# A prologue with fixed instruction queues on three engines, without GpSimd, and with the scale columns as single-column products on TensorE

## The chip, the cores and the metric

The kernel runs on one core of a Trainium2 chip. The metric is the device time of one execution in microseconds (us); the median of three executions is given. Engines are named as in the profile: PE (TensorE), PEld (its weight loads), DVE (VectorE), ACT (ScalarE), POOL (GpSimd) and SP (SyncE, which issues most of the DMAs).

## The reference

One decoder block on a sequence of 1024 tokens with 1024 channels, one sequence, in float32. Two token mixers, a Conformer convolution and an mLSTM, run side by side on one input projection and are merged by gates; a SwiGLU feed-forward block and a final RMS norm follow. What matters here is the start:

```python
mod = silu(c) @ w_ada + b_ada              # (1, 6*1024), six rows of 1024
sh1, sc1, g1, sh2, sc2, g2 = split(mod, 6)
h = rms_norm(x, norm_mix_g) * (1 + sc1) + sh1
proj = h @ w_in + b_in                     # (1024, 10248)
a = proj[:, :1024] * sigmoid(proj[:, 1024:2048])   # then a 31-tap causal convolution
```

Before the first product of `h` with `w_in` can run, the kernel needs the mean square of each token, `x` transposed, and the two conditioning rows `sh1` and `sc1`, each a product of the vector `silu(c)` with a 1024 x 1024 part of `w_ada`.

## The kernel before

The kernel keeps `h` transposed: 8 tiles of 128 channels by 1024 tokens. To keep float32 accuracy at the speed of the faster product format, every operand is split into a high part in that format (`hh`, `whi`) and a low remainder (`hl`, `wlo`), and a product of two matrices becomes three: high by high, high by low, low by high. A block of 128 output channels (`wblock`, line 371) is 8 k-tiles x 3 products x 2 halves of 512 tokens, 48 products, into a two-bank accumulator `mm` of which there are two.

The order of instructions on each engine is chosen by the tile scheduler, which simulates the program with the place in the program as the priority. Code can fix an order with `queue_behind` (line 174), which makes one instruction follow another in its engine's queue without a semaphore wait. The prologue before uses none of that.

The prologue (lines 179 to 320) goes like this.

- Loads: `c`, the four `xt` tiles of `x` (1 MB each), `b_ada`, then the conditioning weights `wad` in four groups of 2 MB (`load_ada`, line 197, four DMAs each: halves of k by shift and scale), with the raw weights of the first two blocks between group 0 and group 1, and the raw weights of the next two blocks (`w_next`, line 217) after group 3. All are issued by SP.
- Mean squares on ACT (line 234), the power for the inverse root on POOL (line 105), the scaling of `xt` on DVE and ACT (line 243, 241), transposes on PE (line 247) and their evacuation to `xT` by ACT or DVE (lines 250 and 252, chosen by `EVAC`).
- The first weights `wf` are split by ACT (high) and POOL (low), lines 149 and 150.
- For each group g of two k-tiles: `mod_cols` (line 263) sums `wad` times `silu(c)` over the 8 k-tiles on DVE, shift and scale together, in eight steps over 128 x 512 (lines 271 and 273), folds the 128 partitions with four single-column products on PE (line 275), and ACT makes the columns `sh1` and `G1` (lines 278 and 279). Then ACT writes `hh` (line 309) and the full value over `xT` (line 313), and the remainder `hl` is subtracted on POOL for k-tiles 0 and 1 and on DVE for the others (line 314).
- `first_products` (line 281) adds the two k-tiles of a group into the accumulators of the first two blocks: 24 products of 128 x 512 a group. In the program those of group g-1 stand behind group g's columns.
- The parameter rows for later (`later`, line 296) share a buffer tag with the sums (`macc`).

After it `glu(1, w_next)` runs the next two blocks, whose weights had been loaded in the prologue and whose low parts POOL subtracts (`WN`). From then on the blocks follow each other, with the convolution taps on DVE put in between by `pump`.

Of the kernel before, what the change touches and what calls it, by code (L numbers as in the profile page):

```python
# [23 lines left out]
PUMP = 5500  # L24
# [25 lines left out]
def hybrid_block(ctx: ExitStack, tc: tile.TileContext, x, c, w_ada, b_ada, norm_mix_g, w_in, b_in,  # L50
                 conv_dw_w, conv_dw_b, conv_ln_g, conv_ln_b, w_conv_pw, b_conv_pw, qk_conv_w,
                 qk_conv_b, mlstm_norm_g, w_out, norm_ffn_g, w_ffn_up, w_ffn_down, final_norm_g, out):
    nc = tc.nc
    PSUM = bass.MemoryType.PSUM
    x2, out2 = x[0], out[0]
    wada, win, wpw, wo = w_ada[0], w_in[0], w_conv_pw[0], w_out[0]
# [81 lines left out]
    def load_raw(src, row0, kt, col0):  # L138
        raw = wp.tile([128, kt, 128], F32, name="wraw", tag="wraw")
        nc.sync.dma_start(raw, src[row0:row0 + kt * 128, col0:col0 + 128].rearrange("(k p) e -> p k e", p=128))  # L140
        return raw

    def load_split(src, row0, kt, col0, hi=None, lo=None, raw=None, eng=None):
        if raw is None:
            raw = load_raw(src, row0, kt, col0)
        if hi is None:
            hi = wp.tile([128, kt, 128], F32R, name="whi", tag="whi")
            lo = wp.tile([128, kt, 128], F32R, name="wlo", tag="wlo")
        nc.scalar.activation(hi, raw, AF.Copy)  # L149
        (eng or nc.vector).tensor_sub(lo, raw, hi.bitcast(F32))  # L150
        return hi, lo
# [43 lines left out]
    wad = []  # L195
# [29 lines left out]
    def dw_col(j, ct):  # L225
        r = j * 8 + ct
        return cols["dw0"][:, r:r + 1] if r < 128 else cols["dw1"][:, r - 128:r - 127]

    rstd = pro.tile([128, 3, 8], F32, name="rstd")
    xT = [big.tile([128, S], F32, name=f"xT{k}", tag="xb") if k < XB else pro.tile([128, S], F32, name=f"xT{k}") for k in range(KT)]  # L230
    for q in range(2):
        for t in range(4 * q, 4 * q + 4):
            junk = ps_mm()
            nc.scalar.activation(flat(junk), xt[t], AF.Square, accum_out=rstd[:, 0, t:t + 1])
        ms, rs, sc = (rstd[:, i, 4 * q:4 * q + 4] for i in range(3))
        nc.vector.tensor_scalar(ms, ms, 1.0 / D, EPS, op0=OP.mult, op1=OP.add)
        rsqrt(rs, ms)
        for t in range(4 * q, 4 * q + 4):
            r = rstd[:, 1, t:t + 1]
            if SCALE[t] == "a":  # L240
                nc.scalar.activation(xt[t], xt[t], AF.Copy, scale=r)
            else:
                (nc.gpsimd if SCALE[t] == "p" else nc.vector).tensor_scalar(xt[t], xt[t], r, None, op0=OP.mult)
        for k in range(KT):
            p = ps_n() if k % 3 == 0 else ps_c()
            for t in range(4):
                nc.tensor.transpose(p[:, t * 128:(t + 1) * 128], xt[q * 4 + t][:, k * 128:(k + 1) * 128], ident)
            h = xT[k][:, q * 512:(q + 1) * 512]
            if EVAC[q][k] == "a":
                nc.scalar.activation(h, p, AF.Copy)  # L250
            else:
                nc.vector.tensor_copy(h, p)

    first = [ps_mm(), ps_mm()]

# [7 lines left out]
    def mod_cols(g):  # L263
        p = ps_a()
        part = lambda t, i: t[:, i // 2, (i % 2) * 128:(i % 2) * 128 + 128]
        b = mod_b[:, g]
        acc = pro.tile([128, 2, 2, 256], F32, name="macc", tag="macc", bufs=MACC)
        for k in range(KT):
            a = acc[:, 0]
            if k < 1:  # L270
                nc.vector.tensor_scalar(a, wad[g][:, k], sc_c[:, k:k + 1], None, op0=OP.mult)
            else:
                nc.vector.scalar_tensor_tensor(a, wad[g][:, k], sc_c[:, k:k + 1], a, op0=OP.mult, op1=OP.add)
        for i in range(4):
            nc.tensor.matmul(p[:, i:i + 1], part(acc[:, 0], i), ones_col, start=True, stop=True)
        for i in range(2):
            k = 2 * g + i
            nc.scalar.activation(sh1[:, k:k + 1], p[:, i:i + 1], AF.Identity, bias=b[:, 0, i:i + 1])
            nc.scalar.activation(G1[:, k:k + 1], p[:, 2 + i:3 + i], AF.Identity, scale=mix_g[:, g, i:i + 1], bias=b[:, 1, i:i + 1])

    def first_products(g):
        ks = (2 * g, 2 * g + 1)
        steps = [(i, k, n, x) for n, x in ((0, hh), (1, hh), (0, hl)) for k in ks for i in range(2)]
        if g == 3:
            steps.sort(key=lambda step: step[0])
        for i, k, n, x in steps:
            for a, b in HALVES:
                nc.tensor.matmul(flat(first[i])[:, a:b], w_first[i][n][:, k, :], x[k][:, a:b], start=(g == 0 and k == 0 and n == 0 and x is hh),
                                 stop=(g == 3 and k == KT - 1 and x is hl))

    hl = []
    for g in range(4):
        mod_cols(g)
        if g == 2:
            rows = pro.tile([128, 8, 128], F32, name="rows", tag="macc", bufs=MACC)
# [11 lines left out]
        ks = (2 * g, 2 * g + 1)  # L307
        for k in ks:
            nc.scalar.activation(hh[k], xT[k], AF.Identity, bias=sh1[:, k:k + 1], scale=G1[:, k:k + 1])
        for k in ks:  # L310
            h = xT[k]
            hl.append(big.tile([128, S], F32R, name=f"hl{k}", tag="xb"))
            nc.scalar.activation(h, h, AF.Identity, bias=sh1[:, k:k + 1], scale=G1[:, k:k + 1])
            (nc.gpsimd if k in ON_POOL else nc.vector).tensor_sub(hl[k], h, hh[k].bitcast(F32))
        if g > 0:
            first_products(g - 1)
    first_products(3)
    for rows in later:
        param_columns(rows)
    prologue.close()  # L320
# [47 lines left out]
    cv = {}  # L368
    done = set()

    def wblock(col0, busy=PUMP, raw=None):
        w = load_split(win, 0, KT, col0, raw=raw, eng=WN if raw is not None else None)
        acc = ps_mm()
        for k in range(KT):
            mm_k(acc, k, KT, w, hh, hl)
            pump(busy / KT)
            yield
        return acc

    def run(steps):  # L380
        for _ in steps:
            pass
# [9 lines left out]
                next(filler, None)  # L392
                credit -= 1

    def glu(ct, raws=(None, None)):
        pb = yield from wblock(GLU_B + ct * 128, raw=raws[0])
        sg = glu_gate(ct, pb)
        pa = yield from wblock(ct * 128, raw=raws[1])
# [890 lines left out]
```

## Time and profile before

| what | value |
|---|---|
| median of three executions | 1737.80 us (1737.73 to 1738.36) |
| the profiled execution's own time | 1740.02 us |
| its span | 1738.3 us, 20880 instructions |
| PE busy, whole span | 1694.6 us (97%) |
| DVE, ACT, POOL busy, whole span | 1253.1, 612.6, 67.6 us |
| first hh product on PE (line 288) | 33.42 us |
| first product of the block after the prologue (line 159) | 67.98 us |
| DMA in the first 44 us | mostly 290 to 420 GB/s |

Times in the profile count from the start of the span. A line such as L273 is a line of the kernel, a group is all instructions of one line, engine and shape, and a pair `out<-in` names the tiles. `x8` is the number of instructions in a row or group. The granted clock is the share of PE's full clock that the throttle let through.

### The profile page before, as it was taken

The page shows a single profiled execution, that of the slowest core. Times are in us where ns is not written, and L with a number is a line of the kernel's source. Part 1 is how long each engine was busy: PE and PEld are TensorE (multiplying, and loading weights), DVE is VectorE, ACT ScalarE, POOL GpSimd, SP SyncE. Part 2 cuts the span into 40 slices and gives each one's busy share as a digit, 9 for nine tenths or more (in the row PEclk, how much of TensorE's full clock was granted, in tenths as well). Part 3 has the DMA queues.
Part 4 walks back from the last instruction along what each step waited for, and adds up shares of the span by engine and source line. Part 5 has one row for each costly group of instructions (what it writes and reads, how often), then busy time and mean ns, then how long its engine had stood idle before and what let it go on. Part 6 is the DMA issues. An engine that isn't in the chain of part 4 may idle for free. (4 is left out here: it accounts for less than half of the span.)

```text
span 1738.3 us, 20880 instructions
## 1 busy us (share of the span) xinstructions
PE 1694.6 (97%) x8360; PEld 1420.8 (82%) x8360; DVE 1253.1 (72%) x1673; ACT 612.6 (35%) x811; POOL 67.6 (4%) x119
## 2 busy tenths in 40 slices
PE   5999999999999999999999998999999999999998
PEld 4798888888888888888888788888888888878887
DVE  7888998997799669537798668766666665685243
ACT  6525335322522253223522376322223221332122
POOL 3100001000001000000000000000000000000000
PEclk8999999999999999999999999999999999999999
DMA  9111111121111111243595642322222222553121
GB/s 334 48 52 46 49 61 38 49 73 61 37 49 61 61 49 48 85 138 91 202 376 188 219 158 98 110 73 85 85 85 73 83 81 97 212 170 112 58 92 53
DMA packets 194711, 179.91 MB, mean 104 GB/s; under 512 B 7463, under 2 KB 166711, under 8 KB 194615
## 3 DMA queue, kind: packets, MB, share of 16 engines
q1 hardware_dynamic: 177367, 146.61, 27.3%
q10 hardware_dynamic: 17248, 31.99, 5.1%
q8 instruction: 65, 1.06, 0.2%
q14 instruction: 31, 0.25, 0.0%
HBM read 146.06 MB, written 32.51 MB: 103 GB/s over the span
## 5 line engine op out<-in xcount | busy, mean ns | idle before, releaser
L341 DVE SCALAR_TENSOR_TENSOR cacc<-a,col,cacc 128x1024 f32<-128x1024 f32 x240 | 305.6, 1280 | 4.7 <-ACT cacc L339 2.3
L159 PE MATMUL mm<-hh,wlo 128*128 128x512 f32 x864 | 271.5, 392 | 1.2 <-DVE wlo L150 1.2
L159 PE MATMUL mm<-hl,whi 128*128 128x512 f32 x864 | 271.9, 392 | 0.0
L159 PE MATMUL mm<-hh,whi 128*128 128x512 f32 x864 | 270.8, 392 | 0.8 <-ACT t L365 0.8
L159 PEld LDWEIGHTS mm<-hh,wlo 128*128 128x128 f32 x864 | 160.5, 188 | 33.5 <-DVE wlo L150 2.3
L159 PEld LDWEIGHTS mm<-hh,whi 128*128 128x128 f32 x864 | 160.4, 188 | 32.6 <-ACT t L365 1.2
L159 PEld LDWEIGHTS mm<-hl,whi 128*128 128x128 f32 x864 | 160.7, 188 | 32.1 <-issue 0.5
L149 ACT ACTIVATE whi<-wraw 128x1024 fp32r<-128x1024 f32 x62 | 65.7, 1060 | 225.0 <-PE mm L159 182.2
L150 DVE TENSOR_TENSOR wlo<-wraw,whi 128x1024 fp32r<-128x1024 f32 x60 | 73.1, 1218 | 22.2 <-ACT whi L149 18.8
L1066 PE MATMUL mm<-Bh,gh 128*128 128x512 f32 (+1 forms) x192 | 71.5, 374 | 3.6 <-ACT gh L1003 3.5
L1067 PE MATMUL mm<-Bl,gh 128*128 128x512 f32 (+1 forms) x192 | 71.5, 373 | 0.6 <-DVE Bl L985 0.6
L556 PE MATMUL mm<-wlo,hh 128*128 128x256 f32 x256 | 72.0, 282 | 0.0
L1068 PE MATMUL mm<-Bh,gl 128*128 128x512 f32 (+1 forms) x192 | 71.2, 371 | 0.0
L487 DVE SCALAR_TENSOR_TENSOR cacc<-qkraw,col,cacc 128x1024 f32<-128x1024 f32 x48 | 61.5, 1281 | 5.3 <-ACT cacc L485 4.6
L1255 DVE TENSOR_TENSOR x<-x,mm 128x1024 f32<-128x1024 f32 x24 | 29.2, 1217 | 50.0 <-PE mm L1253 48.0
L1131 ACT ACTIVATE whi<-wraw 128x512 fp32r<-128x512 f32 (+2 forms) x32 | 25.3, 790 | 111.8 <-PE mm L1253 69.9
L555 PE MATMUL mm<-whi,hh 128*128 128x256 f32 x192 | 54.4, 284 | 0.0
L557 PE MATMUL mm<-whi,hl 128*128 128x256 f32 x192 | 54.2, 283 | 0.0
L1252 PE MATMUL mm<-fa,wlo 128*128 128x512 f32 x128 | 50.1, 391 | 1.0 <-DVE wlo L1132 1.0
L1251 PE MATMUL mm<-fa,whi 128*128 128x512 f32 x128 | 49.9, 390 | 0.9 <-DVE cu L1094 0.9
L1004 DVE TENSOR_TENSOR ul<-uraw,uh 128x1024 fp32r<-128x1024 f32 x20 | 24.5, 1225 | 35.2 <-ACT uh L1003 35.2
L1253 PE MATMUL mm<-fa,whi 128*128 128x512 f32 x128 | 49.8, 389 | 0.0
(442 smaller groups left out, 3917.9 us busy)
## 6 DMA issues: line engine op xcount, KB each, us to landing
wraw<-in_w_in_dram SPq DMA_DIRECT2D x64, 512.0 KB, 4.2
awt<-in_w_ada_dram SPq DMA_DIRECT2D x32, 512.0 KB, 10.1
graw<-in_w_ffn_up_dram SPq DMA_DIRECT2D x24, 512.0 KB, 4.6
uraw<-in_w_ffn_up_dram SPq DMA_DIRECT2D x22, 512.0 KB, 14.5
draw<-in_w_ffn_down_dram SPq DMA_DIRECT2D x22, 512.0 KB, 4.4
act_d<-cg ACTq DMA_DIRECT2D x38, 256.0 KB, 2.2
wad<-in_w_ada_dram SPq DMA_DIRECT2D x16, 512.0 KB, 10.3
wraw<-in_w_out_dram SPq DMA_DIRECT2D x16, 512.0 KB, 3.9
```

Of the source, the lines that this page charges most:

```text
L149: nc.scalar.activation(hi, raw, AF.Copy)
L150: (eng or nc.vector).tensor_sub(lo, raw, hi.bitcast(F32))
L159: nc.tensor.matmul(flat(acc)[:, a:b], lhs[:, k, :], rhs[k][:, a:b], start=(first and k == 0), stop=(last and k == kt - 1))
L341: nc.vector.scalar_tensor_tensor(acc, a[:, j:j + S], dw_col(j, ct), acc, op0=OP.mult, op1=OP.add)
L487: nc.vector.scalar_tensor_tensor(cv, raw[:, j:j + S], wcol(j), cv, op0=OP.mult, op1=OP.add)
L555: nc.tensor.matmul(o, hh[k][:, ts_], his[k], start=False, stop=False)
L556: nc.tensor.matmul(o[:, 0:256], hh[k][:, ts_], los[k], start=False, stop=False)
L557: nc.tensor.matmul(o, hl[k][:, ts_], his[k], start=False, stop=(k == KT - 1))
L1066: nc.tensor.matmul(o, a, rh, start=(k == 0), stop=False)
L1067: nc.tensor.matmul(o, a, rl, start=False, stop=False)
L1068: nc.tensor.matmul(o, b, rh, start=False, stop=(k == 3))
L1252: nc.tensor.matmul(o, lo[:, i, :], his[i][:, a:b], start=False, stop=False)
```

## The change

- `ON_POOL`, `WF` and `WN` go: GpSimd does no subtraction in the prologue any more. The low parts of the first weights and all `hl` are subtracted on DVE.
- The conditioning sums are cut in two. The shift half stays as a sum on DVE (`shift_sums`, over 128 x 256), folded by two single-column products. The scale half is computed on PE directly: for each of the two columns of a group, eight products over k with the `wad` block as the stationary operand and one column of `silu(c)` as the moving one (`mod_products`).
- The full value of the even k-tiles goes to DVE, that of the odd ones stays on ACT.
- `first_products` is cut into the products with `hh` (kind 0, eight pairs) and those with `hl` (kind 1, four pairs).
- `in_turn` fixes the order of the listed groups on DVE (`on_v`), ACT (`on_s`) and PE (`on_t`).
- Only one raw tile of the next pair is loaded in the prologue, in the last group; its split comes last on ACT and DVE, and the pair's second block is loaded and split like any other.
- The parameter rows get their own tag of two buffers.

```diff
-ON_POOL = (0, 1)
-    rows = pro.tile([128, 8, 128], F32, name="rows", tag="macc", bufs=MACC)
+    rows = pro.tile([128, 8, 128], F32, name="rows", tag="rows", bufs=2)
...
-    WF = nc.gpsimd
-    WN = nc.gpsimd
-    w_first = []
+    w_first, raws = [], []
     for i in range(2):
-        w_hi, w_lo = (pro.tile([128, KT, 128], F32R, name=f"wf{i}{j}") for j in range(2))
-        w_first.append(load_split(win, 0, KT, GLU_B if i == 0 else 0, w_hi, w_lo, eng=WF))
+        w_first.append([pro.tile([128, KT, 128], F32R, name=f"wf{i}{j}") for j in range(2)])
+        raws.append(load_raw(win, 0, KT, GLU_B if i == 0 else 0))
...
-    w_next = [load_raw(win, 0, KT, GLU_B + 128), load_raw(win, 0, KT, 128)]
+
+    def split_rest():
+        for i in range(2):
+            load_split(None, 0, KT, 0, *w_first[i], raw=raws[i])
...
+            if q and k > 1:
+                late_evac[e].append(ins)
...
+    def in_turn(groups):
+        for a, b in zip(groups, groups[1:]):
+            for ins in b:
+                for earlier in a:
+                    queue_behind(ins, earlier)
+
+    def shift_sums(g):
+        acc = pro.tile([128, 256], F32, name="macc", tag="macc", bufs=MACC)
+        parts = [[], []]
+        for k in range(KT):
+            if k < 1:
+                ins = nc.vector.tensor_scalar(acc, wad[g][:, k, 0], sc_c[:, k:k + 1], None, op0=OP.mult)
+            else:
+                ins = nc.vector.scalar_tensor_tensor(acc, wad[g][:, k, 0], sc_c[:, k:k + 1], acc, op0=OP.mult, op1=OP.add)
+            parts[k // 4].append(ins)
+        return acc, parts
+
+    def mod_products(g, acc):
+        p = ps_a()
+        out = []
+        for i in range(2):
+            for k in range(KT):
+                out.append(nc.tensor.matmul(p[:, 2 + i:3 + i], wad[g][:, k, 1, i * 128:(i + 1) * 128], sc_c[:, k:k + 1],
+                                            start=(k == 0), stop=(k == KT - 1)))
+        for i in range(2):
+            out.append(nc.tensor.matmul(p[:, i:i + 1], acc[:, i * 128:(i + 1) * 128], ones_col, start=True, stop=True))
+        return p, out
...
+    def full(k):
+        if k % 2:
+            return nc.scalar.activation(xT[k], xT[k], AF.Identity, bias=sh1[:, k:k + 1], scale=G1[:, k:k + 1])
+        return nc.vector.tensor_scalar(xT[k], xT[k], G1[:, k:k + 1], sh1[:, k:k + 1], op0=OP.mult, op1=OP.add)
...
+    acc, parts = shift_sums(0)
+    on_v.append(parts[1])
+    on_v.append(late_evac["v"])
+    on_s.append(late_evac["s"])
+    split_rest()
+    p, ins = mod_products(0, acc)
     for g in range(4):
-        mod_cols(g)
+        on_s.append(mod_cols(g, p))
+        ks = (2 * g, 2 * g + 1)
+        hl += [big.tile([128, S], F32R, name=f"hl{k}", tag="xb") for k in ks]
+        for k in ks:
+            on_s.append([high(k)])
+        if g < 3:
+            acc, parts = shift_sums(g + 1)
+            on_v += parts
+        else:
+            w_next[0] = wp.tile([128, KT, 128], F32R, name="whi", tag="whi"), wp.tile([128, KT, 128], F32R, name="wlo", tag="wlo")
+            raw_next = load_raw(win, 0, KT, GLU_B + 128)
+        for k in ks:
+            f = full(k)
+            (on_s if k % 2 else on_v).append([f])
+            if k == KT - 1:
+                on_s.append([nc.scalar.activation(w_next[0][0], raw_next, AF.Copy)])
+            on_v.append([nc.vector.tensor_sub(hl[k], xT[k], hh[k].bitcast(F32))])
+            if k == KT - 1:
+                on_v.append([nc.vector.tensor_sub(w_next[0][1], raw_next, w_next[0][0].bitcast(F32))])
...
+        on_t.append(first_products(g, 0))
+        if g < 3:
+            p, ins = mod_products(g + 1, acc)
+            on_t.append(ins)
+        on_t.append(first_products(g, 1))
+    for groups in (on_v, on_s, on_t):
+        in_turn([x for x in groups if x])
...
-    run(glu(1, w_next))
+    run(glu(1, w_next[0]))
```

More of the change, by code (lines that the diff above doesn't have):

```diff
@@ L227, in dw_col @@
         return cols["dw0"][:, r:r + 1] if r < 128 else cols["dw1"][:, r - 128:r - 127]
+    late_evac = {"v": [], "s": []}
     rstd = pro.tile([128, 3, 8], F32, name="rstd")
@@ L248, in hybrid_block @@
             h = xT[k][:, q * 512:(q + 1) * 512]
[L249 to L252, printed above, removed]
+            e = "s" if EVAC[q][k] == "a" else "v"
+            ins = nc.scalar.activation(h, p, AF.Copy) if e == "s" else nc.vector.tensor_copy(h, p)
+            if q and k > 1:
+                late_evac[e].append(ins)
     first = [ps_mm(), ps_mm()]
@@ L261, in hybrid_block @@
     nc.vector.tensor_mul(mod_b[:, :, 1], mod_b[:, :, 1], mix_g)
-    def mod_cols(g):
-        p = ps_a()
-        part = lambda t, i: t[:, i // 2, (i % 2) * 128:(i % 2) * 128 + 128]
-        b = mod_b[:, g]
[L267 to L275, printed above, removed]
+    def in_turn(groups):
[3 more added lines that the diff above has]
+                    queue_behind(ins, earlier)
@@ L276, in mod_cols @@
+    def mod_cols(g, p):
+        b = mod_b[:, g]
+        out = []
         for i in range(2):
             k = 2 * g + i
-            nc.scalar.activation(sh1[:, k:k + 1], p[:, i:i + 1], AF.Identity, bias=b[:, 0, i:i + 1])
-            nc.scalar.activation(G1[:, k:k + 1], p[:, 2 + i:3 + i], AF.Identity, scale=mix_g[:, g, i:i + 1], bias=b[:, 1, i:i + 1])
-    def first_products(g):
+            out.append(nc.scalar.activation(sh1[:, k:k + 1], p[:, i:i + 1], AF.Identity, bias=b[:, 0, i:i + 1]))
+            out.append(nc.scalar.activation(G1[:, k:k + 1], p[:, 2 + i:3 + i], AF.Identity, scale=mix_g[:, g, i:i + 1], bias=b[:, 1, i:i + 1]))
+        return out
@@ L282, in first_products, with high @@
+    def high(k):
+        return nc.scalar.activation(hh[k], xT[k], AF.Identity, bias=sh1[:, k:k + 1], scale=G1[:, k:k + 1])
+    def full(k):
+        if k % 2:
+            return nc.scalar.activation(xT[k], xT[k], AF.Identity, bias=sh1[:, k:k + 1], scale=G1[:, k:k + 1])
+        return nc.vector.tensor_scalar(xT[k], xT[k], G1[:, k:k + 1], sh1[:, k:k + 1], op0=OP.mult, op1=OP.add)
+    def first_products(g, kind):
         ks = (2 * g, 2 * g + 1)
-        steps = [(i, k, n, x) for n, x in ((0, hh), (1, hh), (0, hl)) for k in ks for i in range(2)]
@@ L284, in first_products @@
-        if g == 3:
+        x = hl if kind else hh
+        steps = [(i, k, n) for n in ((0,) if kind else (0, 1)) for k in ks for i in range(2)]
+        if g == 3 and kind:
             steps.sort(key=lambda step: step[0])
[L286 to L289, printed above, removed]
@@ L291, in hybrid_block @@
-    hl = []
-    for g in range(4):
-        mod_cols(g)
+        return [nc.tensor.matmul(flat(first[i])[:, a:b], w_first[i][n][:, k, :], x[k][:, a:b],
+                                 start=(g == 0 and k == 0 and n == 0 and not kind), stop=(g == 3 and k == KT - 1 and kind == 1))
+                for i, k, n in steps for a, b in HALVES]
+    on_v, on_s, on_t = [], [], []
+    w_next = [None]
+    hl = []
+    acc, parts = shift_sums(0)
+    on_v.append(parts[1])
+    on_v.append(late_evac["v"])
@@ L294, in hybrid_block @@
         if g == 2:
-            rows = pro.tile([128, 8, 128], F32, name="rows", tag="macc", bufs=MACC)
+            rows = pro.tile([128, 8, 128], F32, name="rows", tag="rows", bufs=2)
             later = [
@@ L306, in hybrid_block @@
             nc.sync.dma_start(bif, bass.AP(tensor=b_in.tensor, offset=b_in.offset + IF0, ap=[[0, 128], [1, 8]]))
[L307 to L317, printed above, removed]
+        on_t.append(first_products(g, 0))
[5 more added lines that the diff above has]
+        in_turn([x for x in groups if x])
     for rows in later:
@@ L369, in hybrid_block, with wblock @@
     done = set()
-    def wblock(col0, busy=PUMP, raw=None):
-        w = load_split(win, 0, KT, col0, raw=raw, eng=WN if raw is not None else None)
+    def wblock(col0, busy=PUMP, w=None):
+        if w is None:
+            w = load_split(win, 0, KT, col0)
         acc = ps_mm()
@@ L393, in mix, with glu @@
                 credit -= 1
-    def glu(ct, raws=(None, None)):
-        pb = yield from wblock(GLU_B + ct * 128, raw=raws[0])
+    def glu(ct, w=None):
+        pb = yield from wblock(GLU_B + ct * 128, w=w)
         sg = glu_gate(ct, pb)
-        pa = yield from wblock(ct * 128, raw=raws[1])
+        pa = yield from wblock(ct * 128)
         glu_post(ct, pa, sg)
     glu_post(0, first[1], glu_gate(0, first[0]))
-    run(glu(1, w_next))
+    run(glu(1, w_next[0]))
     shape4 = [128, 2, 4, 4]
```

## The prediction

> **What bounds the kernel now.** I began with the page's busy shares and the granted clock by slice, then took the first 80 us in stretches of ten.
>
> ```profile
> PE 1694.6 (97%) x8360; PEld 1420.8 (82%) x8360; DVE 1253.1 (72%) x1673; ACT 612.6 (35%) x811; POOL 67.6 (4%) x119
> ...
> PEclk8999999999999999999999999999999999999999
> ```
>
> ```profile
> 20.00:30.00 10.00, 5.80 (x42) 5.04 (x40) 9.86 (x11) 6.06 (x10) 5.12 (x2) 0.90 1.13 332
> 30.00:40.00 10.00, 7.88 (x30) 6.57 (x29) 9.79 (x13) 5.42 (x8) 4.22 (x2) 0.59 1.09 349
> 50.00:60.00 10.00, 9.10 (x40) 6.95 (x38) 9.82 (x7) 5.45 (x10) 4.88 (x2) 0.91 0.46 108
> 70.00:80.00 10.00, 10.00 (x46) 8.29 (x45) 9.17 (x10) 2.47 (x5) 0.33 (x1) 1.00 0.00 0
> 68.00:1730.00 1662.00, 1647.96 (x8145) 1383.45 (x8146) 1200.88 (x1600) 563.92 (x736) 47.29 (x99) 1.00 0.31 98
> ```
>
> Columns after the stretch and its length: busy PE, weight load, DVE, ACT, POOL, granted clock, DMA share, GB/s. From 68 us to the end PE is busy 1648 of 1662 us, so the kernel's time moves one for one with the moment at which PE enters that dense stretch. Before it, DVE is the full engine (9.8 of each 10 us from 20 to 60 us), while PE has gaps and half a clock.
>
> Why DVE is full shows in the groups of the first 70 us:
>
> ```profile
> L273 DVE SCALAR_TENSOR_TENSOR macc<-wad,sc_c,macc 128x512 f32<-128x512 f32 x28 | 32.4, 1164 | 0.6
> L314 DVE TENSOR_TENSOR hl<-xT,hh 128x1024 fp32r<-128x1024 f32 x6 | 7.3, 1220 | 0.7 <-ACT xT L313 0.5
> L314 POOL TENSOR_TENSOR hl<-xT,hh 128x1024 fp32r<-128x1024 f32 x2 | 5.4, 2720 | 7.7 <-DVE rows L116 7.7
> L150 POOL TENSOR_TENSOR wlo<-wraw,whi 128x1024 fp32r<-128x1024 f32 x2 | 5.8, 2919 | 8.5 <-ACT whi L149 8.5
> ```
>
> The conditioning sums take 32.4 us in 28 steps, mean 1164 ns. In order of time, single steps stretch to 2.6 to 2.9 us exactly where POOL runs a 2.5 to 3 us subtraction:
>
> ```profile
> 22.63 0.68 DVE L252 COPY xT<-pc 128x512 f32<-128x512 f32 x1
> 23.23 2.60 DVE L273 SCALAR_TENSOR_TENSOR macc<-wad,sc_c,macc 128x512 f32<-128x512 f32 x1
> 45.22 2.98 DVE L273 SCALAR_TENSOR_TENSOR macc<-wad,sc_c,macc 128x512 f32<-128x512 f32 x4
> ```
>
> Undisturbed, four take 2.98 us, 0.75 each. 28 x 0.75 = 21, so POOL's presence costs DVE about 11 us. The chain that closes the prologue:
>
> ```profile
> 53.20 4.45 DVE L273 SCALAR_TENSOR_TENSOR macc<-wad,sc_c,macc 128x512 f32<-128x512 f32 x3
> 57.99 0.94 PE L275 MATMUL pa<-ones_col,macc 128*128 128x1 f32 x8
> 58.97 0.26 ACT L278 ACTIVATE sh<-pa,mod_b 128x1 f32<-128x1 f32 x1 [4.55 <-PE pa L275]
> 59.75 2.39 ACT L309 ACTIVATE hh<-xT,sh,G 128x1024 fp32r<-128x1024 f32 x2
> 61.22 1.18 PE L288 MATMUL mm<-hh,wf 128*128 128x512 f32 x4
> 62.26 3.01 PE L288 MATMUL mm<-hh,wf 128*128 128x512 f32 x12
> 65.14 2.08 PE L288 MATMUL mm<-hl,wf 128*128 128x512 f32 x8
> 67.98 0.73 PE L159 MATMUL mm<-hh,whi 128*128 128x512 f32 x2 [0.75 <-ACT t L365]
> ```
>
> DVE's last sum ends at 57.65, PE folds it by 58.93, ACT makes the coefficients and the first hh, PE resumes at 61.22, ends the first products at 67.22 and is in the dense part at 67.98.
>
> **The change part by part.** The sum runs to that last moment, T1 = 67.98 now.
>
> *DVE and POOL.* POOL loses its four subtractions; DVE takes over five of 1.22 us (two of the first weights, two hl, one of the next weights), plus four scale-and-shift passes, nearest the 0.68 us copy above (128x512), bounded by 0.68 and 1.28 (the page's 128x1024 two-operand form): 4 to 5 us. The sums shrink from 512 to 256 columns: half of 0.75 if time goes with columns, all of it at worst; I take 0.40, nearest the halving, so 3.2 us a group. From 19.7 us DVE then has 13 (sums) + 2 (evacuations) + 2.4 (weights) + 3 (three passes by then) + 4.9 (four hl) = 25 us to the end of the fourth sum, 45 us; bounds 40 to 57. The conditioning weights land by about 43:
>
> ```profile
> L202 SPq DMA_DIRECT2D wad<-in_w_ada_dram x16: 385/1416/2649, 4.2 to 32.4; - x16
> DMA to landing us min/median/max: 8.0/10.3/10.8
> ```
>
> (last issue 32.4 + 10.3). The saving of some 12 us of DVE end is real, but it only counts as far as PE can follow.
>
> *PE, added.* Per group, 16 single-column products over k plus two folds, against four folds before. The trace has this very form (a weight load of 128x128 and one column), eight records for four products, since each f32 product is two:
>
> ```profile
> 29.43 1.78 PEld L275 LDWEIGHTS pa<-ones_col,macc 128*128 128x128 f32 x8 [1.66 <-DVE macc L273]
> 46.02 1.05 PE L275 MATMUL pa<-ones_col,macc 128*128 128x1 f32 x8 [2.38 <-DVE macc L273]
> 57.77 1.08 PEld L275 LDWEIGHTS pa<-ones_col,macc 128*128 128x128 f32 x8
> ```
>
> 1.05/8 to 1.08/8 is 0.13 with the tail, 0.11 without; at half clock 1.78/8 = 0.22. I take 0.12: 36 records are 4.3 us a group (bounds 4.0 and 8.0). Accumulating over k in one column is not new: both records of one product already do.
>
> *PE, fixed order.* The queue is now: products with hh of group g, single-column products of g+1, products with hl of g, hh of g+1. So nothing of group g+1 on ACT starts before 3.7 us of hh products and 4.3 us of single columns have run in series. From the first hh product, T0, at full clock: 96 products at 0.23 ((3.01-0.39)/11 is 0.238, dense part 0.227) = 22; three stretches of 4.3 = 13; three waits for ACT, each 61.22-58.93 = 2.3 less 8 hl products (1.8) = 0.5, together 1.5; four waits of 0.3 for a group's second hh (1.2 against 0.9 of products); 0.8 from the last product to the dense part. Sum 38.5. Before, T0 to T1 took 67.98-33.42 = 34.6 us, throttled clock and all. So the path behind T0 has grown by 4 and all gain must come from T0.
>
> *T0.* ACT's queue now holds mod_cols(0) behind the late evacuations:
>
> ```profile
> 21.80 1.05 ACT L149 ACTIVATE wf<-wraw 128x1024 fp32r<-128x1024 f32 x1
> 28.05 0.60 ACT L250 ACTIVATE xT<-pn 128x512 f32<-128x512 f32 x1 [0.27 <-PE pn L247]
> 31.34 0.26 ACT L278 ACTIVATE sh<-pa,mod_b 128x1 f32<-128x1 f32 x1 [2.69 <-PE pa L275]
> 33.42 6.12 PE L288 MATMUL mm<-hh,wf 128*128 128x512 f32 x16 [2.12 <-ACT hh L309]
> ```
>
> Without DVE's stalls: from 21.8, two splits (2.1), five evacuations (3.0), coefficients (0.8), first hh (1.2) = 28.9. If the first group's 4.3 us of single columns run after the transposes (about 25.5), it is 29.8 + 2.3 = 32.1; if they fill earlier gaps, 28.9. I take 30.5. T1 = 30.5 + 38.5 = 69.0, that is +1.0, at full clock.
>
> *The clock.* Here the trace speaks against the change. The clock falls and rises at:
>
> ```profile
> 27.60:28.00 0.40, 0.40 (x4) 0.18 (x2) 0.40 (x1) 0.18 (x1) 0.40 (x1) 0.88 1.09 348
> 38.00:38.40 0.40, 0.40 (x3) 0.36 (x2) 0.40 (x1) 0.00 (x0) 0.40 (x1) 0.82 1.09 348
> 48.20:48.50 0.30, 0.30 (x3) 0.26 (x2) 0.30 (x2) 0.30 (x1) 0.00 (x0) 0.80 0.06 14
> 51.50:51.80 0.30, 0.30 (x3) 0.20 (x1) 0.30 (x1) 0.30 (x1) 0.09 (x1) 0.51 0.00 0
> ```
>
> at 27.9, 38.1, 48.3 and 51.8, distances of 10.2, 10.2 and 3.4: a grid of 3.41 us. PE's busy time in three grid intervals, then the single-column products' share of the last:
>
> ```profile
> 24.44:27.85 3.41, 1.38 (x13) 1.29 (x12) 3.41 (x3) 1.47 (x3) 3.41 (x2) 1.00 1.09 348
> 41.50:44.92 3.42, 2.14 (x8) 1.12 (x7) 3.28 (x6) 3.42 (x4) 0.00 (x0) 1.00 1.09 259
> 44.92:48.33 3.41, 2.31 (x14) 2.11 (x15) 3.34 (x6) 2.07 (x6) 0.00 (x0) 1.00 0.15 36
> ...
> 44.92:48.33 3.41, 1.05 (x8) 0.97 (x8) 1.00 0.15 36
> ```
>
> After 1.38 the clock halves, after 2.14 it stays, yet after 2.31, of which 1.05 are single columns, it halves. This fits if single columns count for little: 1.3 to 1.4 then, like the first. A stretch of 4.3 us is longer than the grid, so each would cost about one interval at half clock, 3.4 x 0.5 = 1.7 us: three stretches, 5.1 (0 if single columns count in full; 13.6 if two intervals fall to each of four stretches). I take 5.1, total +6.1.
>
> [...]
>
> *The rest.* The rows tile in a tag of its own only frees its DMAs of a wait; they are still behind the conditioning weights on SP. The second block of the next pair loses its early load and POOL split: it is loaded and split (1.1 on ACT, 1.2 on DVE) under the 11 us of the block before it; uncovered, it would cost 2.3. The next weights' low half is last on DVE, 1.2 us after the last hl, covered by 0.5 us of products and 1.3 us of evacuation.
>
> **The rivals.** (a) *Full clock throughout*: single columns count as work. For it: the interval 38.09 to 41.50 holds 0.95 us of them and stays fast. Against: the three rows above. +1.0 (bounds -1.8 with T0 28.9 and 0.11 a record, to +5 with T0 32.1 and 0.13), 1738.8: no change. (b) *Cheap products*: 32 in a row pipeline better than 8, 0.06 each; 13 becomes 6.5, the clock stays full: -5.5, 1732.3, faster. Against: 0.11 to 0.13 in all four groups. (c) *A stalled fixed queue*: the late evacuations on DVE stand behind the second half of the first sum, so behind its DMA; if that lands near 27 instead of 20, transposes, T0 and T1 move by 5 to 7 more: 1750. Against: the first half is consumed at 16.6 today.
>
> **How the numbers follow.** Halved clock 0.55, (a) 0.29, (b) 0.10, (c) 0.06. The profiled execution took 1740.02 with a span of 1738.28, 2.2 above the median 1737.80; I add differences to the median: 1737.8 + 6.1 = 1743.9, the profiled one 1746.1. Measurement tells 0.2%, 3.5 us, from nothing. Forecast alone: 1740.5 to 1751 (1.0 + 1.7 to 13.6, little of its end kept). With (a) and most of (b): 1734.0 to 1751. Faster 0.13 (0.09 of b, 0.04 of a), same 0.28 (0.23 of a, the rest from the edges), slower 0.59.
>
> **What would show it.** Right: sums near 0.4 us with none over 1 us; L275-form products of 4.3 us or more a group; PE's first hh product at 29 to 32; granted clock near 0.5 for several 3.4 us intervals between 28 and 70; PE's dense part from 72 to 78. Wrong: clock 1.00 from 35 on, or DVE again 9.8 of 10 at 50 us, or a product record under 0.09.

## The result and the profile after

| what | before | after |
|---|---|---|
| median | 1738.47 us (9 executions) | 1750.69 us (9 executions, 1744.2 to 1754.18) |
| ratio after to before | | 1.0062, 95% interval 1.0046 to 1.0079 |
| span of the profiled execution | 1738.3 us | 1746.5 us |
| first hh product on PE | 33.42 us | 37.31 us |
| first product of the dense part | 67.98 us | 80.47 us |
| from there to the end | 1670.30 us | 1666.05 us |

The changed kernel is slower by 0.62%, 10.8 us by the ratio and 12.2 us by the medians. The dense part begins 12.5 us later. The profiled execution shows only 8.2 us of this, since its dense part happened to be 4.2 us shorter; the reason follows below.

The page's busy shares and clock after:

```profile
PE 1713.0 (98%) x8472; PEld 1440.6 (82%) x8472; DVE 1244.5 (71%) x1683; ACT 609.0 (35%) x807; POOL 51.5 (3%) x113
...
PEclk9899999999999999999999999999999999999999
```

The stretches of ten (busy PE, weight load, DVE, ACT, POOL, granted clock, DMA share, GB/s):

```profile
20.00:30.00 10.00, 10.00 (x51) 10.00 (x50) 5.27 (x8) 4.84 (x7) 0.00 (x0) 1.00 1.12 332
30.00:40.00 10.00, 7.40 (x32) 6.62 (x32) 6.10 (x12) 6.68 (x11) 0.00 (x0) 0.86 1.09 348
40.00:50.00 10.00, 10.00 (x57) 8.77 (x56) 6.98 (x12) 3.27 (x7) 0.00 (x0) 0.84 0.50 136
50.00:60.00 10.00, 10.00 (x57) 8.80 (x57) 5.84 (x11) 3.31 (x7) 0.00 (x0) 0.84 0.07 17
60.00:70.00 10.00, 10.00 (x57) 9.05 (x56) 3.15 (x3) 2.58 (x4) 0.00 (x0) 0.84 0.00 0
70.00:80.00 10.00, 9.83 (x35) 7.48 (x33) 6.09 (x8) 7.91 (x10) 0.19 (x2) 0.76 0.24 68
```

The roles have changed over. DVE, full before, is at 3 to 7 of 10 us; PE has no idle time from 40 to 70 us, at a clock of 0.84. (The 1.00 of the first row is no measurement; the last section says why.) PE in order of time (start, length, engine, line, operation):

```profile
17.77 1.71 PE L286 MATMUL pa<-sc_c,wad 128*128 128x1 f32 x8
21.07 1.06 PE L248 MATMUL pn<-ident,xt 128*128 128x128 f32 x4
24.77 1.95 PE L248 MATMUL pc<-ident,xt 128*128 128x128 f32 x8
34.10 0.60 PE L248 MATMUL pn<-ident,xt 128*128 128x128 f32 x4
37.31 5.44 PE L315 MATMUL mm<-hh,wf 128*128 128x512 f32 x16 [2.60 <-ACT hh L302]
42.59 3.63 PE L286 MATMUL pa<-sc_c,wad 128*128 128x1 f32 x32
46.08 0.58 PE L289 MATMUL pa<-ones_col,macc 128*128 128x1 f32 x4
46.52 3.03 PE L315 MATMUL mm<-hl,wf 128*128 128x512 f32 x8
49.35 4.52 PE L315 MATMUL mm<-hh,wf 128*128 128x512 f32 x16
...
80.47 0.73 PE L158 MATMUL mm<-hh,whi 128*128 128x512 f32 x2
```

Two things are to be seen. A stretch of single-column products and folds takes 4.1 us (42.59 to 46.66), at full clock, and the products behind it are slow: eight hl products in 3.03 us against 2.08 in the kernel before's last group. And up to 34 us the transposes themselves run at half pace, 1.95 us for eight, with the first group's product records between them from 17.77 to 30 us; only at 34.10 do four take 0.60. ACT waits for them, not for DVE:

```profile
31.24 0.60 ACT L251 ACTIVATE xT<-pc 128x512 f32<-128x512 f32 x1 [2.28 <-PE pc L248]
35.24 0.26 ACT L297 ACTIVATE sh<-pa,mod_b 128x1 f32<-128x1 f32 x1
```

The sums on DVE are no longer stretched, but a step of 256 columns takes 485 ns, not half of 750 (minimum, median, maximum):

```profile
L277 DVE SCALAR_TENSOR_TENSOR macc<-wad,sc_c,macc x28: 478/485/486, 16.3 to 55.8; 128x256 f32<-128x256 f32 x28
```

**The 4.2 us of the dense part.** They lie around the change from the output projection to the feed-forward block. PE's wait there, and what the DVE chain ahead of it waited for, first in the kernel before:

```profile
1039.88 0.69 DVE L962 TENSOR_TENSOR x<-x,mm 128x512 f32<-128x512 f32 x1 [4.25 <-DMA x<-in_x_dram]
...
1047.55 0.39 PE L1066 MATMUL mm<-Bh,gh 128*128 128x256 f32 x1 [3.51 <-ACT gh L1003]
```

and after:

```profile
1049.36 0.69 DVE L1013 TENSOR_TENSOR x<-x,mm 128x512 f32<-128x512 f32 x1 [1.83 <-DMA x<-in_x_dram]
...
1057.04 0.38 PE L1117 MATMUL mm<-Bh,gh 128*128 128x256 f32 x1 [1.10 <-ACT gh L1054]
```

A load that came 2.4 us less late took 2.4 us from PE's wait, and the half-clock interval that followed the long wait before (1048.4 to 1051.8) did not occur, which is another 1.7 us (half of 3.4). Over all profiles of this study the dense part took 1666.0 to 1673.7 us without any order that follows the prologue; why is not settled, and a single profile's span is not a measure of the prologue for that reason. The start of the dense part and the ratios are used below, and neither is exact: the start comes from one execution of each kernel.

### The profile page after: what moved, and what is told of

It reads as the page before. It is cut to its first block, busy times and chain, and to the rows that moved or that the text cites. A ratio compares the mean times of both kernels' runs of the same rounds, so it can differ in the third digit from the quotient of the medians.

```text
span 1746.5 us, 21098 instructions
## 1 busy us (share of the span) xinstructions
PE 1713.0 (98%) x8472; PEld 1440.6 (82%) x8472; DVE 1244.5 (71%) x1683; ACT 609.0 (35%) x807; POOL 51.5 (3%) x113
## 5 line engine op out<-in xcount | busy, mean ns | idle before, releaser
L158 PEld LDWEIGHTS mm<-hl,whi 128*128 128x128 f32 x864 | 160.7, 188 | 32.1 <-issue 0.5
L1055 DVE TENSOR_TENSOR ul<-uraw,uh 128x1024 fp32r<-128x1024 f32 x20 | 24.5, 1225 | 34.8 <-ACT uh L1054 34.8
```

The costliest lines, as they stand in the source:

```text
L158: nc.tensor.matmul(flat(acc)[:, a:b], lhs[:, k, :], rhs[k][:, a:b], start=(first and k == 0), stop=(last and k == kt - 1))
```

## The experiments

Theory A: the scale columns on PE cost the time, in three ways: they stand in series with the products that wait for them, they lower the clock, and those of the first group delay the first hh product. Rival B: the fixed queues themselves. Each experiment was timed beside the kernel before; ratios are to that kernel, with a 95% interval. A profile shows one execution.

**All sums back on DVE.** The fixed queues, the empty POOL and the late split stay.

```diff
-        acc = pro.tile([128, 256], F32, name="macc", tag="macc", bufs=MACC)
+        if g in (0, 1, 2, 3):
+            acc = pro.tile([128, 2, 256], F32, name="macc2", tag="macc2", bufs=2)
+            src = wad[g]
...
-                ins = nc.vector.scalar_tensor_tensor(acc, wad[g][:, k, 0], sc_c[:, k:k + 1], acc, op0=OP.mult, op1=OP.add)
+                ins = nc.vector.scalar_tensor_tensor(acc, src[:, k], sc_c[:, k:k + 1], acc, op0=OP.mult, op1=OP.add)
...
+        if g in (0, 1, 2, 3):
+            for i in range(4):
+                out.append(nc.tensor.matmul(p[:, i:i + 1], acc[:, i // 2, (i % 2) * 128:(i % 2) * 128 + 128], ones_col, start=True, stop=True))
+            return p, out
```

> All four groups sum shift and scale on DVE again (steps over 128 x 512, four folds on PE); the fixed queues and the empty POOL stay. Theory A (the single-column products cost the time: 13 us in series on PE, the half-clock intervals they bring, and the late first group): the first hh product moves from 37.3 to 29-31 us, DVE has about 5.8 us a group and ends the fourth sum near 54, the dense part starts at 61-65, kernel 1732 to 1737, faster than before. Rival B (the fixed queues themselves, whatever they hold, make the prologue late): the dense part stays later than before's 68, kernel 1742 to 1750.

Ratio 0.998 (0.9969 to 0.999), median 1736.0 us: faster than both kernels. The dense part begins at 64.1 us.

```profile
30.92 6.75 PE L324 MATMUL mm<-hh,wf 128*128 128x512 f32 x16 [2.12 <-ACT hh L311]
53.29 1.05 PE L291 MATMUL pa<-ones_col,macc 128*128 128x1 f32 x8 [1.09 <-DVE macc L282]
```

The first hh product is at 30.92, and PE waits for DVE's sums again (1.09 us ahead of the last folds). Rival B falls: with the same fixed queues the kernel is some 14 us faster than the changed one, and the edit moves the scale columns and nothing else.

**The same once more**, beside later runs:

> The version with all sums on DVE once more, beside the divisions: 1735 to 1737, 0.1 to 0.3% under the kernel before.

Ratio 0.9985 (0.9975 to 0.9994), median 1736.08; this profile's dense part begins at 65.6. The gain over the kernel before is small, and it came twice.

**128 columns in place of one.** The moving operand is the same column, repeated.

```diff
-                out.append(nc.tensor.matmul(p[:, 2 + i:3 + i], wad[g][:, k, 1, i * 128:(i + 1) * 128], sc_c[:, k:k + 1],
+                out.append(nc.tensor.matmul(p[:, 128 + i * 128:256 + i * 128], wad[g][:, k, 1, i * 128:(i + 1) * 128], sc_c[:, k:k + 1].to_broadcast([128, 128]),
...
```

> The moving operand of the scale products is the column repeated 128 times, so 128 columns of each product instead of one; the results read are the same. Theory A1 (a product with one moving column hardly counts as work for the clock): a record stays near 0.11-0.12 us at full clock, but the granted clock stays 1.00 from about 25 us on; the first hh product comes at 31-34, the dense part at 69-72, kernel 1738 to 1742, faster than the changed kernel although PE does 128 times as much. Rival (the clock falls for the waits of PE on ACT, or the products only cost their time): half-clock intervals as in the changed kernel, kernel at or above its time, 1748 to 1756.

Ratio 1.0015 (1.0006 to 1.0024), median 1741.07: of the 0.62% that the change costs, 0.47 points are gone, with 128 times as much arithmetic in these products. PE in order of time:

```profile
21.05 0.63 PE L248 MATMUL pn<-ident,xt 128*128 128x128 f32 x4
31.42 5.49 PE L315 MATMUL mm<-hh,wf 128*128 128x512 f32 x16 [2.60 <-ACT hh L302]
36.75 3.73 PE L286 MATMUL pa<-sc_c,wad 128*128 128x128 f32 x32
```

and its stretches of ten:

```profile
40.00:50.00 10.00, 9.84 (x61) 8.19 (x60) 6.70 (x12) 4.40 (x7) 0.00 (x0) 1.00 0.48 127
50.00:60.00 10.00, 9.85 (x60) 8.15 (x60) 3.73 (x4) 4.41 (x7) 0.00 (x0) 1.00 0.10 24
60.00:70.00 10.00, 9.72 (x48) 7.31 (x47) 6.21 (x9) 8.57 (x11) 0.25 (x4) 1.00 0.07 12
```

32 records take 3.73 us instead of 3.63, the clock is 1.00 from 40 us on instead of 0.84, and the first hh product is 5.9 us earlier, since the transposes too found the full pace: here four take 0.63 us at 21.05, in the changed kernel 1.06 at 21.07. This separates the clock from the order: the queues and the records are the same. That the single columns lower the clock is shown: in the profiles of the changed kernel and of the next experiment, half clock (0.50) follows each of the six stretches of 32 single-column records; here, at 1.00, it follows none of the three.

**Only the first group on DVE.** The condition of the first edit for group 0 alone.

> Only group 0 sums its scale columns on DVE; groups 1 to 3 keep the products on PE. It isolates the late first hh product. Theory A: the transposes are no longer interleaved with 32 product records at half clock, the first hh product comes at 30-31 instead of 37.3, the rest as in the changed kernel, kernel 5 to 7 us under it (1742 to 1745). Rival (the start is late for another reason, DMA or ACT): first hh product still at 36 or later.

Ratio 1.0049 (1.0034 to 1.0064), median 1748.49, 2.2 us under the changed kernel, less than the 5 to 7 expected, and the two intervals overlap. The profile has the expected mechanism:

```profile
30.92 5.54 PE L324 MATMUL mm<-hh,wf 128*128 128x512 f32 x16 [2.12 <-ACT hh L311]
47.45 3.63 PE L295 MATMUL pa<-sc_c,wad 128*128 128x1 f32 x32
```

The first hh product is at 30.92 and the dense part at 74.2, 6.3 earlier than after. So the late first group is a cost in the profiles; over the executions a saving of 2 us is not clear of the noise, and 6 us cannot be ruled out. Why the medians show less than the profiles is open.

**Only groups 1 to 3 on DVE.** The same condition for groups 1 to 3 (and one buffer, not three, for group 0's sum).

> Groups 1 to 3 sum on DVE, group 0 keeps its products on PE. It isolates the three serial stretches. Theory A: first hh product still near 37, from there 31 us or so to the dense part instead of 43, dense part at 67-70, kernel 1737 to 1741. Rival B (fixed queues): from the first hh product to the dense part still 38 or more.

Ratio 1.0022 (1.0011 to 1.0032), median 1742.93, above the 1737 to 1741 expected: 7.8 us under the changed kernel, still 0.42 points over the version with all sums on DVE.

```profile
16.76 0.66 PE L248 MATMUL pn<-ident,xt 128*128 128x128 f32 x4 [0.97 <-ACT xT L251]
26.24 1.12 PE L248 MATMUL pc<-ident,xt 128*128 128x128 f32 x4 [0.72 <-DVE xT L251]
32.86 5.54 PE L324 MATMUL mm<-hh,wf 128*128 128x512 f32 x16 [2.60 <-ACT hh L311]
```

From the first hh product to the dense part (67.0) it takes 34.1 us instead of 43.2: the three serial stretches, with the half clock that they bring, are 9 us in the profile. Here, with the same products of group 0 between the transposes, the transposes had full pace before the first of these products (0.66 for four at 16.76), lost it for one interval at 26 us (1.12 for four), and the first hh product came at 32.86, not near 37 as expected. The pace at the start differs between profiles of programs that are alike up to there: in the two divisions below, which differ only behind the first group, four transposes take 0.66 us at 16.95 (128 columns) and 1.11 at 16.83 (one). With no products between the transposes the first hh product came at 30.93 and 30.81 in those two; with single columns between them it came at 32.86 here, after the fast start, and at 37.31 in the changed kernel, after a slow one (1.12 for four at 16.86).

**PE's queue left to the scheduler**, in the changed kernel (`for groups in (on_v, on_s)`).

> The changed kernel with the PE queue left to the scheduler (DVE and ACT stay fixed). Theory A (the cost is in the products and the clock, not in the order of the queue): the scheduler puts the products of a group a little earlier, the stretches and the half-clock intervals stay, kernel 1746 to 1752, within 4 us of the changed one. Rival (the fixed PE order makes the series): kernel 1738 to 1743.

Ratio 1.0095 (1.0081 to 1.011), median 1753.66 of four executions, just above the range expected: not the fixed PE order; without it the kernel is slower still. The scheduler splits the stretches and puts hh products behind single columns of the next group; the profile has 20 us of half clock in the prologue from its first recorded change on, 17 in the changed kernel. The profiled execution is the fastest of the four, and its dense part begins at 76.0, before the changed kernel's 80.5, so the profile does not account for the median.

**No fixed queue at all**, in the version with all sums on DVE.

> The version with all sums on DVE, without any fixed queue. It tells what the fixed queues are worth by themselves. Theory (they neither cost nor gain much): within 2 us of that version, 1734 to 1738. Rival B (the fixed queues cost): 1729 to 1733. If they gain: 1739 to 1743.

Ratio 1.005 (1.0038 to 1.0062), median 1747.43, 11 us over the same version with fixed queues. This was not expected by any theory; the third case, a gain of the queues, was priced at half of it. The place, ACT in order of time:

```profile
49.92 1.06 ACT L353 ACTIVATE whi<-wraw 128x1024 fp32r<-128x1024 f32 x1 [5.87 <-DMA wraw<-in_w_in_dram]
52.56 0.24 ACT L306 ACTIVATE sh<-pa,mod_b 128x1 f32<-128x1 f32 x1
```

and behind it on PE:

```profile
55.89 2.08 PE L324 MATMUL mm<-hl,wf 128*128 128x512 f32 x4 [5.25 <-DVE hl L354]
```

The scheduler puts the split of the next pair's weights ahead of the third group's coefficients on ACT; its load, issued behind the parameter rows, lands at 50, and ACT, then DVE, then PE stand for 5 to 6 us. Putting that split last is worth its place in the change. These waits are about half of the 11 us; the dense part begins at 73.7, 8 to 10 us later. Which of the three queues is worth how much was not tested.

**POOL's six subtractions on DVE**, alone, in the kernel before (`ON_POOL = ()`, `WF` and `WN` on `nc.vector`).

> The kernel before with POOL's six subtractions of the prologue moved to DVE and nothing else (the first group's sums and the early loads stay). Theory (POOL's subtractions stretch DVE's sums by about 11 us, more than the 7.3 us that six subtractions of 1.22 cost): DVE's sum steps at 0.75 with none over 1 us, dense part at 63 to 67 instead of 68, kernel 1734 to 1738, level or up to 4 us faster. Rival (POOL was worth having): DVE later, dense part at 70 or more, kernel 1740 to 1746.

Ratio 1.0011 (1.0002 to 1.002), median 1740.2; dense part at 69.1 in the profile, 1.1 later. Neither range was met in full: the stretched sums are gone (none over 753 ns), and the gain is eaten, it seems, by the subtractions and by the order that the scheduler then chose. To leave POOL without work gained nothing by itself.

**Extra products that keep PE at work.** In the version with all sums on DVE, ten products of 128x512 between the first folds and the first hh product.

```diff
+    spare = w_first[0][0].rearrange("p k e -> p (k e)")
+    on_t.append([nc.tensor.matmul(flat(first[i % 2])[:, 0:512], w_first[0][0][:, 0, :], spare[:, 0:512], start=True, stop=True) for i in range(10)])
```

> The version with all sums on DVE, and ten extra products of 128x512 on PE between the first group's folds and its first hh product, into an accumulator that the real products start afresh; they only keep PE at work in its 2.1 us wait. Theory (the clock follows the work of the last 3.4 us interval): fewer half-clock intervals in the prologue (none or one where the version without them had two), the first 16 hh products in 3.8 to 5 us instead of 6.75, the dense part at 61 to 63 us, kernel 1732.5 to 1735, 1 to 3 us under the version without them. Rival (the clock does not hang on such work): same clock, 10 products more on PE, kernel level or up to 2 us slower.

Ratio 1.0004 (0.9995 to 1.0012), median 1739.04: slower by 3 us where a gain was expected.

```profile
28.46 3.82 PE L339 MATMUL mm<-wf 128*128 128x512 f32 x10
32.07 4.18 PE L324 MATMUL mm<-hh,wf 128*128 128x512 f32 x16
45.86 3.40 PE L324 MATMUL mm<-hl,wf 128*128 128x512 f32 x8 [0.93 <-DVE hl L357]
55.08 1.19 PE L324 MATMUL mm<-hl,wf 128*128 128x512 f32 x4 [0.93 <-DVE hl L357]
```

The mechanism worked at its place: the first 16 products take 4.18 us instead of 6.75. But DVE sets the pace (its fourth sum ends at 53.0, against 53.2 without the extra products), PE comes early to waits for it, and the clock fell again at 46.5 and at 56.7. That makes three half-clock intervals in the prologue, against two and three in the two profiles without the extra products (the second fell at 56.6 too). A faster PE ahead of a full DVE won nothing. The dense part begins at 65.8, against 64.1 and 65.6, so where the median's 3 us lie is not settled.

**A division between DVE and PE.** Group 0 on DVE; in the others DVE sums 384 columns and PE makes the last 128, with 128 columns moved, and in a second run with one.

```diff
+            if g:
+                for k in range(KT):
+                    out.append(nc.tensor.matmul(p[:, 3:131], wad[g][:, k, 1, 128:256], sc_c[:, k:k + 1].to_broadcast([128, 128]), start=(k == 0), stop=(k == KT - 1)))
+            for i in range(3 if g else 4):
+                out.append(nc.tensor.matmul(p[:, i:i + 1], acc[:, i * 128:i * 128 + 128], ones_col, start=True, stop=True))
```

> A division between the two: group 0 wholly on DVE; in groups 1 to 3 DVE sums three quarters (384 columns) and PE makes the last quarter as eight products with the column repeated to 128. DVE's group goes from 9.2 to about 7.8 us, PE gets 16 records (1.9 us) more a group. Theory (the version with all sums on DVE is bound by DVE, its fourth sum ends at 53, and products of 128 columns do not lower the clock): fourth sum at 49 to 51, dense part at 61 to 63, kernel 1732 to 1735, the fastest of all. Rival (PE's series is the bound already): no gain, 1736 to 1739.

> The same division with single-column products, 16 records and three folds in a row, 2.3 us, less than one 3.4 us interval. Theory (single columns count for little, but a stretch shorter than the interval need not lower the clock each time): one or two more half-clock intervals than with 128 columns, kernel 0 to 4 us over it, 1733 to 1738.

128 columns: ratio 1.0019 (1.001 to 1.0027), median 1742.11. DVE's fourth sum ends at 50.4, as expected, but the dense part begins at 66.0, for PE is the bound at once:

```profile
45.88 1.94 PE L292 MATMUL pa<-sc_c,wad 128*128 128x128 f32 x16
47.66 0.73 PE L294 MATMUL pa<-ones_col,macc 128*128 128x1 f32 x6
```

Each group's 2.5 us stand in front of its coefficients, whatever DVE has ready; the rival's mechanism was right, and the time is above both ranges.

One column: ratio 1.0006 (0.9998 to 1.0015), median 1740.15, level with the kernel before, and above its range too. In the clock the pair repeats what the long stretches showed. One grid interval with a single-column stretch and the interval behind it:

```profile
45.22:48.63 3.41, 3.41 (x28) 3.24 (x27) 3.23 (x7) 0.34 (x2) 0.00 (x0) 1.00 0.53 138
48.63:52.05 3.42, 3.42 (x9) 2.63 (x8) 3.11 (x5) 3.39 (x6) 0.00 (x0) 0.50 0.70 182
```

Half clock follows each of the three stretches with one column and none with 128: the profile has four half-clock intervals (13.7 us) against two (6.8), and its dense part begins at 67.9. In time the pair does not repeat it: one column is 2 us faster in the medians. The dense parts of these two profiles differ the other way, 1671.2 us against 1673.7, and why is open. So to keep the clock did not pay for these short stretches.

**32 columns**, in the changed kernel.

> The changed kernel with the column repeated 32 times, a quarter of the 128. If the clock goes by the columns that are moved, a stretch of these counts as a quarter of work and the half-clock intervals stay: kernel 1747 to 1753, like single columns. If it goes by instructions that move more than one column, it behaves like 128: 1739 to 1743.

Ratio 1.0045 (1.0029 to 1.0061), median 1748.73, the time that was expected for "like single columns". The profile is not so simple. One grid interval of the changed kernel, then the interval behind it; all instructions, then the products alone:

```profile
44.03:47.45 3.42, 3.42 (x28) 3.27 (x28) 1.95 (x5) 0.75 (x4) 0.00 (x0) 1.00 0.23 49
47.45:50.86 3.41, 3.41 (x10) 2.63 (x9) 2.04 (x2) 3.38 (x4) 0.00 (x0) 0.50 1.01 275
```

```profile
44.03:47.45 3.42, 2.18 (x20) 2.10 (x19) 1.00 0.23 49
```

and the answering ones with 32 columns:

```profile
44.46:47.88 3.42, 3.42 (x29) 3.27 (x29) 1.94 (x4) 0.70 (x4) 0.00 (x0) 1.00 0.29 64
47.88:51.29 3.41, 3.26 (x14) 2.09 (x13) 2.01 (x2) 3.38 (x4) 0.00 (x0) 1.00 0.95 258
```

```profile
44.46:47.88 3.42, 2.26 (x21) 2.15 (x20) 1.00 0.29 64
```

The same records, the same share of the interval, PE busy throughout in both: after single columns the clock halves, after 32 columns it stays. But before 34 us the transposes with 32-column products between them were as slow as with one (1.95 us for eight at 24.83, as at 24.77 there), and the first hh product came at 37.70. So in this profile 32 columns were enough to keep the full clock and not to reach it. From the first hh product to the dense part (76.6) it takes 38.9 us, as with 128 columns (38.8), so the whole difference between these two profiles lies ahead of the first hh product. How many columns that takes, and whether the median's 7.7 us over 128 columns is all from the start, is open.

## Why the prediction was right, and where it was not

**The bound and the one-for-one rule: right, within the 8 us by which the dense part varies between profiles.** Its start moved by 12.5 us and the medians by 12.2. That these agree so closely is luck: the two profiled executions themselves differ by 8.2 us. The median of 1750.7 lies at the end of the forecast range of 1740.5 to 1751.

**DVE: right in kind, mis-sized without effect.** The stretched sums are gone with POOL's work (no step over 486 ns, where they reached 2.9 us). A sum step cost 0.485 us, not 0.40, and the fourth sum ended at 56.3 us instead of 45, since it now stands behind hl subtractions that wait, by way of ACT, for PE. DVE was not the bound. (POOL lost six subtractions, not four; nothing in the sum hung on it.)

**The price of the products: right.** 36 records in 4.1 us at full clock against 4.3.

**The path behind T0: right in its sum and in its mechanism, with luck in the sum.** Predicted 38.5 us and 5.1 for the clock, 43.6; measured 80.47 - 37.31 = 43.2. The clock fell at the end of each product stretch or just behind it, at 47.4, 57.7 and 67.9, the last time for two intervals, as the rows of the kernel before had suggested, and the 128-column run shows that it was the single columns. But with the interval at 37.2, behind the 2.6 us wait for the first hh, there were five intervals at half clock where the forecast had three: 3.4 us more at its own price of 1.7 each. Against that, the waits for ACT that it put at 2.7 us (1.5 and 1.2) did not occur: between 37.3 and 80.5 PE is idle for 0.4 us alone, just ahead of the dense part. The two errors nearly cancel.

**T0: wrong, and it is the term that made the size off.** I took 30.5, between 28.9 (the first group's single-column products all in earlier gaps, at no cost) and 32.1 (all behind the transposes). Both ends suppose that the products do not slow the transposes. In the profile the products stand between the transposes, PE is busy from 17 to 34 us almost without a gap, and the pace stays half; it rises only at 34 us, after the first grid interval with transposes alone, and the first hh product came at 37.3. With 128 columns in the same places, after a start that was as slow (1.11 us for four at 16.73 against 1.12 at 16.86), the transposes had full pace at 21.05 (0.63 for four). Where full pace had come before the products, as in the run with only groups 1 to 3 on DVE, the first hh product came at 32.9. The dense part moved by 12.5 us against 6.1 forecast, a miss of 6.4: T0 was 6.8 too early in the forecast, and the path behind it 0.4 too long. Two of the signs that were to show the forecast right failed with it: the first hh product at 29 to 32, and the dense part from 72 to 78. In medians the late first group is worth 2 us with the other groups on PE, which the noise covers, and 6.9 with them on DVE (1742.93 - 1736.0).

**Rival (a), full clock throughout: fell**; but with 128 columns moved it came near, 1.0015 (1.0006 to 1.0024) against the +1.0 us (0.06%) that it gave. (Its bounds, added up again from the terms that it names, are -1.6 and +3.8, not -1.8 and +5.) **Rival (b), cheap products: fell**, 32 in a row cost 0.11 us a record. **Rival (c), a stalled queue: fell in its form**; the late evacuations did wait, but for the transposes on PE, not for a DMA. Its size was nearer than the forecast's: it moved T0 by 5 to 7 us more and gave 1750. It got there by another cause, with a chance of 0.06.

**Idle gaps and the clock.** In the changed kernel PE has no idle time from 40 to 70 us, at a clock of 0.84: busy records alone did not hold the clock. Nor is it shown that an idle gap lowered it at 48.3 in the kernel before: the interval with the 2.4 us wait ahead of 46.02 also held 1.05 us of single columns. A fall without them is in the run with POOL's subtractions on DVE, behind an interval in which PE worked 1.21 us, between two waits of 1.6 and 1.7 us:

```profile
47.62:51.03 3.41, 1.21 (x4) 0.67 (x4) 3.41 (x4) 3.41 (x8) 0.00 (x0) 1.00 0.49 115
51.03:54.45 3.42, 2.82 (x7) 2.24 (x8) 3.28 (x5) 3.06 (x3) 0.00 (x0) 0.50 0.88 216
```

**What the parts are worth.** From the version with all sums on DVE: the scale columns as single-column products +0.82 points (0.998 to 1.0062), of which 0.47 go when 128 columns are moved. The 0.35 that are left I put down to the series on PE: from the first hh product to the dense part it takes 38.8 us with 128 columns, 33.2 and 34.8 in the two profiles with all sums on DVE. The fixed queues are worth -0.7 points (1.005 to 0.998). The version that keeps the queues and the late split and leaves the sums on DVE is the fastest, 0.2% under the kernel before.

## What to carry to other kernels

Before moving work from a full engine to PE, ask what stands in series with it there and what it does to the clock: here stretches of products with one moving column kept PE busy for 4.1 us each, and a clock of 0.50 followed each. If a long stretch of such products must be made on PE, try the column repeated; here 128 moved columns cost 0.1 us more in 3.7 and kept the clock at 1.00. For stretches of 2.5 us the repeat kept the clock too and gained no time (1.0019 against 1.0006). And judge a bundle by its parts: here the fixed queues gained 0.7 points and the moved products lost 0.8.

## What the runs showed of the hardware that was not expected

- The clock row of a profile reads 1.00 before its first recorded change, while the transposes of the changed kernel take 1.95 us for eight (1.07 for eight at 25.87 with 128 columns moved): up to there it is not a measurement, and the pace of a repeated record is.
- The pace of the transposes rose with nothing but transposes on PE. In the kernel before, four take 1.11 us at 16.8 and 0.60 at 21.5, with no other product between:

```profile
16.80 1.11 PE L247 MATMUL pn<-ident,xt 128*128 128x128 f32 x4 [0.97 <-ACT xT L250]
21.54 0.60 PE L247 MATMUL pn<-ident,xt 128*128 128x128 f32 x4
```

- A DVE step on half the columns (256 of 512) took 485 ns against 750, so 65%, not 50%.
- The changed kernel's executions spread over 10 us (1744.2 to 1754.18), the kernel before's over 6.6 (1737.27 to 1743.88). That this is the place of the 3.4 us grid (the clock changes at 37.2, 40.6, 47.4 and 50.8 us in the changed kernel) against the product stretches is argued from the differing starts above, not shown.
